# Hybrid streaming encoder on one core: the small products of the mixers' beside-work come one large product later

## The chip, the cores and the metric

The kernel runs on one core of a Trainium2 chip. The metric is the device time of one execution in microseconds (us), lower is better; a kernel's time is the median of several executions. Engines are named as the profile names them: PE (TensorE, matrix products; PEld loads its weights), DVE (VectorE), ACT (ScalarE), POOL (GpSimd), SP (the queue that issues most DMAs).

## The reference

One layer of a hybrid encoder over 2048 prompt rows and 32 rows of a running stream, all in float32, with shared weights:

```python
h = rms_norm(x, g_mix)
p = h @ w_in                              # 1024 -> 2048, eight segments of 256 columns
ya = pool_mixer(seg 0)                    # windows 2/4/8/16, mean - self, 64x64 linear
yb = conformer_conv(seg 1, seg 2)         # GLU, depthwise conv of 31 taps, LayerNorm, silu
yc = short_conv(seg 3, seg 4, seg 5)      # B * conv3(C * x)
yd = chunk_mlp(seg 6, seg 7)              # u * (tril(W_s) v + b), chunks of 128 rows
x = x + concat(ya, yb, yc, yd) @ w_out    # 1024 -> 1024
f = rms_norm(x, g_ffn)
x = x + (silu(f @ w_gate) * (f @ w_up)) @ w_down      # 1024 -> 2816 -> 1024
y = rms_norm(x, g_final)
```

It returns y and the last rows of the mixers' inputs as new states.

## The kernel before

Activations lie transposed: features on the 128 partitions, rows (tokens) along the free side. The 2080 rows make five chunks c0 to c4 of 416. Every float32 product is made of three faster ones: both operands are split into a high part (`hi`, `whi`, a cast on ACT) and the rest (`lo`, `wlo`, a subtraction on POOL or DVE), and PE adds up hi*whi, hi*wlo and lo*whi. A **large product** (`product`, L230 to L232) multiplies one chunk with one block of 128 output columns: 8 depth tiles times 3, 24 matmuls into one PSUM bank of `ps_mm` (five banks).

The chunks go through the mixers in three passes: c0; c1 and c2; c3 and c4. A pass multiplies with the column blocks of `w_in`: v (14, 15), the gated conv (`glu`, 4, 2, 5, 3), the short conv (`short`, 6, 10, 7, 11), pool (0, 1) and the gates (8, 9, 12, 13); the third pass runs in the order v, pool, glu, short, gates. Output passes with `w_out` (`w_out_pass`, eight column blocks) follow: that of c0 after the second pass, that of c1 and c2 and then that of c3 and c4 after the third. Then comes the FFN, a fast matrix scheme with fewer products (PE lines L1138 to L1155).

Beside the large products runs the rest of the mixers' work, as generators in the list `ahead`; `fill(budget)` is called once behind each large product and steps up to three of them until the budget (2.8 or 3.7 us of DVE work) is spent. A `yield` of a number is the cost of what was just issued. A `yield WAIT` ends this generator's turn until the next `fill`, so what follows it is issued at least one large product later. After `yield LATE` the generator is taken up again at the end of the same `fill`. The long conv (`taps`, 30 steps for two column halves, DVE line L727) stands in `spare` and gets what budget is left. `need(names)` runs a generator to its end at once: where a stage must have a result, all that is left is issued there, with no large product between. The order on PE and DVE is that of the program; for ACT, POOL and the DMA queues a scheduler in the compiler lays it down.

The small products of this work go to `ps_ax` (three banks):

- `spatial`: for each 128 rows, `turned` transposes v on PE (`tp`, L621) and copies it out on ACT (`vt`, L625); at the next step `mixed` multiplies it with the chunk weights (`mx`, L632) and DVE adds into `mix` (L646, and for c0 L651). A step issues `mx` of one chunk and `tp` of the next, then a WAIT.
- `pooling`: DVE builds window sums (`sa`, `sb`, L686 to L706), and `multiply` takes them through the 64x64 linear on PE (`pp`, L673).
- `normed_silu`, the LayerNorm after the long conv: `sm` on DVE (L739), `total` on PE (L743), subtract the mean on DVE (L747), squares on ACT (L756) and their sum on POOL (L757), the sums by row on PE (`tok`, L147), `ms` on DVE (L157), the power -1/2 on POOL (`rt`, L163). The scale then goes to all partitions: in the first two passes' chunks by DRAM (`spread_far`, `line` and `rs`), for c3 and c4 by PE (`dg` on DVE L168, `rb` on PE L179). DVE multiplies (L774) and ACT applies silu (L777).
- `ffn_stats`: squares of the output rows (`ssum`, ACT and DVE L347), summed by row on PE (`tok`, L147), the scales stored for the FFN. `first_operands` waits for those of c0 and c1 and then builds the FFN's first operands (DVE L993 to L1014).

`need` stands in four places that matter here: `in_pool` needs `spatial` in the first two passes; `in_short` of the third pass needs `spatial(2)`; `in_gates` needs `pooling` and `normed_silu` of chunks before; and in the output pass of c1 and c2, before its last two column blocks, `taps(2)`, `normed_silu` of c3 and c4 and `pooling(2)` are needed. The rows of x for the next chunk come by DMA (`xk`) to `normed`, which scales them on DVE (`f`, L211).

Of the kernel before, what the change touches and what calls it, by code (L numbers as in the profile page):

```python
# [58 lines left out]
def tail(p):  # L59

    lo, hi = PASSES[p][0] * C, (PASSES[p][-1] + 1) * C
    if hi <= T_PROMPT:
        return hi - lo, 0
    return T_PROMPT - lo, hi - T_PROMPT
# [21 lines left out]
def trunk_kernel(ctx: ExitStack, tc: tile.TileContext, a):  # L86
# [17 lines left out]
    def col(name, i):  # L104
        return par[:, OFF[name] + i : OFF[name] + i + 1]
# [18 lines left out]
    def row(name):  # L124
        return rowp.tile([P, C], F32, tag="row", name=name, bufs=6)
# [17 lines left out]
    def sum_tok(ssum):  # L143

        tok = ps_ax.tile([P, 512], F32, tag="ax", name="tok")
        for j in range(NTB):
            nc.tensor.matmul(  # L147
                tok[:TB, j : j + 1], ssum[:, j * TB : (j + 1) * TB], ones[:, :1], start=True, stop=True
            )
        return tok[:TB, :NTB]  # L150
# [104 lines left out]
    WAIT, LATE, DONE = object(), object(), object()  # L255
# [78 lines left out]
    def ffn_stats(c):  # L334

        acc = row("ssum")
        for ks in (range(6), range(6, KT)):
            while ks[0] and c not in whole:
                yield WAIT
            nc.sync.dma_start(  # L340
                out=x2d[:, ks[0] : ks[-1] + 1, c * C : (c + 1) * C], in_=x2[c][:, ks[0] : ks[-1] + 1]
            )
            for k in ks:
                sq = acc if k == 0 else row("sq")
                nc.scalar.activation(out=sq, in_=x2[c][:, k], func=AF.Square)
                if k:
                    nc.vector.tensor_add(out=acc, in0=acc, in1=sq)  # L347
                    yield 0.55
        made["squares", c] = True
        yield WAIT  # L350
        yield WAIT
        tok = sum_tok(acc)
        yield LATE
        rt = rsqrt_of([tok], 1.0 / D)
        yield WAIT
        nc.sync.dma_start(out=rline[c * NTB : (c + 1) * NTB].rearrange("j q -> q j"), in_=rt[:TB])
# [23 lines left out]
    with ExitStack() as st:  # L380
# [95 lines left out]
        def conv_pieces(p, h, c):  # L476
            return [(s, d - c * C + PASSES[p][0] * C, n) for s, d, n in pieces(p, h)
                    if PASSES[p][0] + d // C == c]
# [127 lines left out]
        def spatial(p, v):  # L606
            first = PASSES[p][0] * C
            n0, n1 = tail(p)
            todo = []
            t0 = first // P * P  # L610
            while t0 < first + n0:
                i0, i1 = max(first - t0, 0), min(P, first + n0 - t0)
                todo.append((HV + t0 - first, i1, i0, t0 + i0 - first))
                t0 += P
            if n1:
                todo.append((HV + n0, n1, 0, n0))

            def turned(src, k, i0, dst):
                tp = ps_ax.tile([P, 512], F32, tag="ax", name="tp")
                for t in range(2):  # L620
                    nc.tensor.transpose(  # L621
                        out=tp[:k, t * P : (t + 1) * P], in_=v[:, t, src : src + k], identity=ident
                    )
                vt = segp.tile([P, 2 * P], F32, tag="vt", name="vt", bufs=2)
                nc.scalar.copy(out=vt[:k], in_=tp[:k, : 2 * P])  # L625
                return vt

            def mixed(vt, src, k, i0, dst):
                mx = ps_ax.tile([P, 2, 2, P], F32, tag="ax", name="mx")
                n = k - i0  # L630
                for t in range(2):
                    nc.tensor.matmul(  # L632
                        mx[:, t, :, :n], vt[:k, t * P : (t + 1) * P], wst[:k, 2 * t : 2 * t + 2, i0:k],
                        start=True, stop=True,
                    )
                return mx

            def added(mx, src, k, i0, dst):
                n = k - i0
                done = 0  # L640
                while done < n:
                    c, o = PASSES[p][0] + (dst + done) // C, (dst + done) % C
                    m = min(n - done, C - o)
                    for j in range(2):
                        q = slice(64 * j, 64 * (j + 1))
                        nc.vector.tensor_add(  # L646
                            out=mix[c][q, 6:8, o : o + m], in0=mx[q, :, j, done : done + m],
                            in1=bsb[q, :, i0 + done : i0 + done + m],
                        )
                    if c == 0:  # L650
                        nc.vector.tensor_mul(  # L651
                            out=mix[c][:, 6:8, o : o + m], in0=mix[c][:, 6:8, o : o + m],
                            in1=rfirst[:, o : o + m].rearrange("p (a n) -> p a n", a=1).broadcast_to([P, 2, m]),
                        )
                    done += m

            vt = None
            for i in range(len(todo) + 1):
                mx = mixed(vt, *todo[i - 1]) if vt else None
                vt = turned(*todo[i]) if i < len(todo) else None  # L660
                yield LATE
                if mx:
                    added(mx, *todo[i - 1])
                    yield 0.7
                yield WAIT

        def pooling(p, pz):
            late = None

            def multiply(c, t, cuts, lo, sa):  # L670
                ps = ps_ax.tile([P, 512], F32, tag="ax", name="pp")
                for s, d, m in cuts:
                    nc.tensor.matmul(  # L673
                        ps[:, d : d + m], wpool[:, t], sa[:, s - lo : s - lo + m], start=True, stop=True
                    )
                nc.scalar.activation(out=mix[c][:, t], in_=ps[:, :C], func=AF.Copy, scale=col("pool_scale", t))

            for c in PASSES[p]:
                cuts = conv_pieces(p, 15, c)
                lo = cuts[0][0] - 15  # L680
                n = cuts[-1][0] + cuts[-1][2] - lo
                for t in range(2):
                    x = pz[:, t, lo : lo + n]
                    sa = segp.tile([P, 30 + C], F32, tag="sum", name="sa", bufs=2)
                    sb = segp.tile([P, 30 + C], F32, tag="sumb", name="sb")
                    nc.vector.tensor_add(out=sa[:, 1:n], in0=x[:, 1:n], in1=x[:, : n - 1])  # L686
                    yield 0.5
                    if t == 1:
                        nc.vector.tensor_add(out=sb[:, 3:n], in0=sa[:, 3:n], in1=sa[:, 1 : n - 2])
                        nc.vector.tensor_add(out=sa[:, 7:n], in0=sb[:, 7:n], in1=sb[:, 3 : n - 4])  # L690
                        yield 1.0
                    w = WINDOWS[2 * t]
                    nc.vector.tensor_add(out=sb[64:, 15:n], in0=sa[64:, 15:n], in1=sa[64:, 15 - w : n - w])
                    yield 0.5
                    fix = segp.tile([P, 15], F32, tag="fix", name="fix", bufs=2) if c == 0 else None
                    for q, s, w in ((slice(0, 64), sa, w), (slice(64, P), sb, 2 * w)):
                        if c == 0:
                            o = OFF["rc"] + 15 * t
                            nc.vector.tensor_mul(out=fix[q], in0=s[q, 15:30], in1=par[q, o : o + 15])
                            nc.vector.tensor_sub(out=fix[q], in0=fix[q], in1=x[q, 15:30])  # L700
                        nc.vector.scalar_tensor_tensor(
                            out=sa[q, 15:n], in0=s[q, 15:n], scalar=1.0 / w, in1=x[q, 15:n],
                            op0=ALU.mult, op1=ALU.subtract,
                        )
                        if c == 0:
                            nc.vector.tensor_copy(out=sa[q, 15:30], in_=fix[q])  # L706
                        yield 0.5
                    if late:
                        multiply(*late)
                    late = c, t, cuts, lo, sa  # L710
            yield WAIT
            multiply(*late)

# [21 lines left out]
        def normed_silu(p, c, cv):  # L735
            pcs = [(s - 30, d, m) for s, d, m in conv_pieces(p, 30, c)]
            sm = row("sm")
            for s, d, m in pcs:
                nc.vector.tensor_add(out=sm[:, d : d + m], in0=cv[:, 0, s : s + m], in1=cv[:, 1, s : s + m])  # L739
            yield 0.5  # L740
            yield WAIT
            total = ps_ax.tile([P, 512], F32, tag="ax", name="total")
            nc.tensor.matmul(total[:, :C], ones, sm, start=True, stop=True)  # L743
# [918 lines left out]
```

## Time and profile before

| what | value |
|---|---|
| time, median of 3 | 2114.95 us (2113.97 to 2116.43) |
| the profiled execution's own time | 2113.76 us |
| its span, first to last instruction | 2112.0 us |
| PE busy | 2028.9 us (96%), 11902 matmuls |
| DVE busy | 1451.7 us (69%) |
| ACT busy | 767.8 us (36%) |
| POOL busy | 1125.0 us (53%) |
| DMA | 247.88 MB, mean 117 GB/s |

The mixers take the first 31% of the span and the FFN the rest. Matmuls are pipelined, so a busy PE is not PE at its peak. Rows of groups read: line, engine, operation, tiles written and read, shape, count, then busy us, mean ns of one, and idle time of the engine before them with what ended it. Rows in order of time read: start, length, engine, line, operation, and in brackets the idle time just before.

### The profile page before, as it was taken

To read this page: it belongs to the slowest core of one execution; us is meant where nothing else is said; L and a number is where in the kernel's file an instruction comes from. 1 tells how busy PE (TensorE), PEld (TensorE's weight loads), DVE (VectorE), ACT (ScalarE), POOL (GpSimd) and SP (SyncE) were. 2 spreads that over 40 slices of the span, in tenths; PEclk is the share of its full clock that TensorE was granted. 3 is DMA by queue.
4 is the path that set the end of the run, shared out by engine and by line. 5 is a ranking of instruction groups with operands and counts; after the bars stand their busy time and mean duration, and the time that the engine had idled before them with its cause. 6 is when DMAs were issued, how large, how long until landed. Compare 5 with 4: busy or idle time off the path is not lost.

```text
span 2112.0 us, 31921 instructions
## 1 busy us (share of the span) xinstructions
PE 2028.9 (96%) x11902; PEld 1989.9 (94%) x11902; DVE 1451.7 (69%) x2245; ACT 767.8 (36%) x1472; POOL 1125.0 (53%) x891
## 2 busy tenths in 40 slices
PE   8799998999998999999998999999998999999997
PEld 8689997899897999999998999999998999999997
DVE  3785599499677678656557576667778576666555
ACT  5424232232334333333334343433334343433332
POOL 2433352243244666656666566655666566656664
PEclk9999998999998999999999999999999999999998
DMA  7633243213267444322223524334444524332221
GB/s 208 176 104 109 65 126 103 50 59 117 99 175 209 137 133 146 109 71 77 76 96 134 193 90 124 111 110 127 147 132 150 192 89 126 111 109 91 76 80 60
DMA packets 152011, 247.88 MB, mean 117 GB/s; under 512 B 23440, under 2 KB 101008, under 8 KB 151216
## 3 DMA queue, kind: packets, MB, share of 16 engines
q1 hardware_dynamic: 149136, 245.67, 37.9%
q8 instruction: 94, 1.54, 0.3%
q10 hardware_dynamic: 2720, 0.18, 0.1%
q14 instruction: 61, 0.50, 0.1%
HBM read 209.42 MB, written 36.36 MB: 116 GB/s over the span
## 4 chain that ended last, share of the span: by engine, by line
PE 67%; DVE 16%; DMA 6%; issue 6%; POOL 4%; ACT 1%; SPq 0%; DVEq 0%; POOLq 0%; ACTq 0%
PE pw L1140 12%; PE pw L1138 12%; PE pw L1139 12%; PE pd L1154 7%; PE pd L1155 7%; PE pd L1153 7%; DVE cv L727 5%; PE ps L232 3%; PE ps L230 3%; PE ps L231 3%; POOL wlo L1024 2%; DVE f_p L965 2%; DMA xk<-in_x 1%; DMA line<-rt 1%; DMA raw<-in_w_in 1%
## 5 line engine op out<-in xcount | busy, mean ns | idle before, releaser
L1138 PE MATMUL pw<-f_p,whi 128*128 128x346 f32 (+1 forms) x1848 | 597.7, 323 | 10.3 <-DVE sg L1231 7.4
L1140 PE MATMUL pw<-f_p,whi 128*128 128x346 f32 (+1 forms) x1848 | 598.0, 324 | 3.7 <-POOL f_p L965 3.7
L1139 PE MATMUL pw<-f_p,wlo 128*128 128x346 f32 (+1 forms) x1848 | 596.3, 323 | 0.0
L1024 POOL TENSOR_TENSOR wlo<-sum,whi 128x512 fp32r<-128x512 f32 x264 | 355.2, 1350 | 292.8 <-ACT whi L1023 284.4
L1156 DVE TENSOR_TENSOR xs<-pd,xs 128x346 f32<-128x346 f32 (+1 forms) x528 | 263.7, 513 | 243.3 <-PE pd L1155 242.7
L1138 PEld LDWEIGHTS pw<-f_p,whi 128*128 128x128 f32 x1848 | 352.3, 191 | 12.0 <-issue 8.6
L1140 PEld LDWEIGHTS pw<-f_p,whi 128*128 128x128 f32 x1848 | 350.5, 190 | 4.9 <-POOL f_p L965 4.9
L1139 PEld LDWEIGHTS pw<-f_p,wlo 128*128 128x128 f32 x1848 | 350.8, 190 | 0.3 <-POOL wlo L1024 0.3
L1153 PE MATMUL pd<-hhi,dhi 128*128 128x346 f32 (+1 forms) x1024 | 330.6, 323 | 10.1 <-DVE xs L1156 10.0
L1281 POOL TENSOR_TENSOR dlo<-raw,dhi 128x256 fp32r<-128x256 f32 x256 | 223.4, 892 | 217.7 <-ACT dhi L1280 212.4
L1154 PE MATMUL pd<-hhi,dlo 128*128 128x346 f32 (+1 forms) x1024 | 329.9, 322 | 0.0
L1155 PE MATMUL pd<-hlo,dhi 128*128 128x346 f32 (+1 forms) x1024 | 329.6, 322 | 0.0
L138 POOL TENSOR_TENSOR wlo<-raw,whi 128x1024 fp32r<-128x1024 f32 x67 | 182.4, 2726 | 271.6 <-ACT whi L137 269.9
L1024 POOL TENSOR_TENSOR wlo<-raw,whi 128x512 fp32r<-128x512 f32 x199 | 279.5, 1412 | 40.7 <-ACT whi L1023 40.7
L1023 ACT CAST whi<-sum 128x512 fp32r<-128x512 f32 x264 | 163.8, 620 | 288.9 <-DVE sum L1061 102.9
L230 PE MATMUL ps<-hi,whi 128*128 128x416 f32 x640 | 238.1, 372 | 7.4 <-ACT hi L214 3.5
L232 PE MATMUL ps<-lo,whi 128*128 128x416 f32 x640 | 233.0, 364 | 3.1 <-POOL lo L207 2.7
L231 PE MATMUL ps<-hi,wlo 128*128 128x416 f32 x640 | 230.9, 361 | 5.2 <-POOL wlo L138 4.7
L727 DVE SCALAR_TENSOR_TENSOR cv<-z,par,cv 128x416 f32<-128x416 f32 (+2 forms) x180 | 213.3, 1245 | 1.1 <-ACT cv L721 0.9
L1153 PEld LDWEIGHTS pd<-hhi,dhi 128*128 128x128 f32 x1024 | 193.4, 189 | 13.3 <-DVE xs L1156 12.2
L1155 PEld LDWEIGHTS pd<-hlo,dhi 128*128 128x128 f32 x1024 | 193.7, 189 | 0.0
L1154 PEld LDWEIGHTS pd<-hhi,dlo 128*128 128x128 f32 x1024 | 193.2, 189 | 0.4
(185 smaller groups left out, 2861.7 us busy)
## 6 DMA issues: line engine op xcount, KB each, us to landing
raw<-in_w_up SPq DMA_DIRECT2D x132, 256.0 KB
raw<-in_w_gate SPq DMA_DIRECT2D x128, 256.0 KB
raw<-in_w_down SPq DMA_DIRECT2D x256, 128.0 KB
raw<-in_w_in SPq DMA_DIRECT2D x43, 512.0 KB
raw<-in_w_out SPq DMA_DIRECT2D x24, 512.0 KB
f_p<-td SPq DMA_DIRECT2D x14, 692.0 KB
xt<-in_xt SPq DMA_DIRECT2D x20, 416.0 KB
x<-in_x SPq DMA_DIRECT2D x5, 1664.0 KB
```

Of the source, the lines that this page charges most:

```text
L230: nc.tensor.matmul(out, whi, xhi, start=start and k == 0, stop=False)
L231: nc.tensor.matmul(out, wlo, xhi, start=False, stop=False)
L232: nc.tensor.matmul(out, whi, xlo, start=False, stop=stop and k == n - 1)
L727: nc.vector.scalar_tensor_tensor(out=cv[:, t, :n], in0=z[:, t, j : j + n], scalar=col("w_conf", 31 * t + j), in1=cv[:, t, :n], op0=ALU.mul ...
L1024: nc.gpsimd.tensor_sub(out=lf, in0=src, in1=hf.bitcast(F32))
L1138: nc.tensor.matmul(ps, whi[:, k], xhi[:, k, :n], start=start and k == 0, stop=False, **more)
L1139: nc.tensor.matmul(ps, wlo[:, k], xhi[:, k, :n], start=False, stop=False, **more)
L1140: nc.tensor.matmul(ps, whi[:, k], xlo[:, k, :n], start=False, stop=stop and k == H - 1, **more)
L1153: nc.tensor.matmul(ps, whi, hhi[:, :n], start=i == 0, stop=False)
L1154: nc.tensor.matmul(ps, wlo, hhi[:, :n], start=False, stop=False)
L1155: nc.tensor.matmul(ps, whi, hlo[:, :n], start=False, stop=i == 1)
L1156: nc.vector.tensor_add(out=xs[c, m], in0=ps, in1=xs[c, m])
```

## The change

Five more `yield WAIT`, in four generators. In `ffn_stats` and `normed_silu` one more stands before the sums (`tok` of the FFN's norm, `total` of the LayerNorm), in `spatial` one more at the end of each step, in `pooling` one more before each `multiply`.

```diff
@@ ffn_stats
         made["squares", c] = True
         yield WAIT
         yield WAIT
+        yield WAIT
         tok = sum_tok(acc)
@@ spatial
                 if mx:
                     added(mx, *todo[i - 1])
                     yield 0.7
+                yield WAIT
                 yield WAIT
@@ pooling
                     if late:
+                        yield WAIT
                         multiply(*late)
                     late = c, t, cuts, lo, sa
+            yield WAIT
             yield WAIT
             multiply(*late)
@@ normed_silu
             yield 0.5
+            yield WAIT
             yield WAIT
             total = ps_ax.tile([P, 512], F32, tag="ax", name="total")
```

The new lines shift the numbers behind them by one to five (L632 is L633 in the changed kernel, L743 is L748, L777 is L782). The matmuls are the same ones; their places differ. Three places show it.

PE in the third pass, the end of `spatial(2)`. Before, its last steps stand between the products of `glu` (here the last two mixings, with a large product between that begins at `ps_3079`):

```order
L632 MATMUL mx_3047<-wst_111,vt_3006 128x256 x2
L621 MATMUL tp_3050<-ident_82,v_2535 32x128 x2
L230 MATMUL ps_3079<-hi_2185,whi_3067 128x416
...
L632 MATMUL mx_3112<-wst_111,vt_3053 128x2x32 x2
L230 MATMUL ps_3119<-hi_2185,whi_3073 128x416
```

Now `need` issues the last three mixings and two transposes in one piece, between the last product of `glu` and the first of `short` (`ps_3230`):

```order
L633 MATMUL mx_3190<-wst_111,vt_3141 128x256 x2
L622 MATMUL tp_3193<-ident_82,v_2535 128x128 x2
L633 MATMUL mx_3200<-wst_111,vt_3196 128x256 x2
L622 MATMUL tp_3203<-ident_82,v_2535 32x128 x2
L633 MATMUL mx_3210<-wst_111,vt_3206 128x2x32 x2
L230 MATMUL ps_3230<-hi_2185,whi_3218 128x416
```

In the same way four mixings and three transposes of `spatial(1)` now follow `total` in one piece before the first product of `in_pool` in the second pass.

ACT at that place of the third pass. Now the two copies that this drain needs (`vt_3196`, `vt_3206`) stand behind the silu activations of c1 and c2 (L782) and behind two DMA issues of the conv's state:

```order
L626 COPY vt_3141<-tp_3138 128x256
L782 ACT_TABLE_LOAD
L782 ACTIVATE mix_1107<-cv_1952,par_80 128x416 x2
L782 ACTIVATE mix_1106<-cv_1952,par_80 128x416 x2
L725 ACTIVATE cv_3263<-z_2845,par_80 128x862
L137 CAST whi_3378<-raw_3380 128x1024
L474 DMA out_o_conv<-z_2845 128x2x30
L475 DMA out_o_conv<-z_2845 128x2x30
L626 COPY vt_3196<-tp_3193 128x256
L725 ACTIVATE cv_3263<-z_2845,par_80 128x862
L626 COPY vt_3206<-tp_3203 32x256
```

Before, the last copy of `spatial(2)` (`vt_3053`) stood ahead of these activations.

PE in the output pass of c1 and c2, the LayerNorm of c3 and c4. Before, totals, sums and spreads each stand behind a large product of their own (two large products lie between the totals and the sums, one between the sums and the spreads):

```order
L743 MATMUL total_4140<-sm_4097,ones_87 128x416
L743 MATMUL total_4142<-sm_4100,ones_87 128x416
L230 MATMUL ps_4163<-mhi_3767,whi_4109 128x416
...
L147 MATMUL tok_4214<-ones_87,q0_4148 104x1 x4
L147 MATMUL tok_4219<-ones_87,q0_4157 104x1 x4
L230 MATMUL ps_4233<-mhi_3834,whi_4109 128x416
...
L179 MATMUL rb_4263<-dg_4260,ones_87 128x416
L179 MATMUL rb_4269<-dg_4258,ones_87 128x416
L230 MATMUL ps_4291<-mhi_3767,whi_4279 128x416
```

Now all of them stand in one piece before the same large product (`ps_4291`):

```order
L748 MATMUL total_4218<-sm_4161,ones_87 128x416
L748 MATMUL total_4220<-sm_4164,ones_87 128x416
L147 MATMUL tok_4241<-ones_87,q0_4235 104x1 x4
L179 MATMUL rb_4252<-dg_4250,ones_87 128x416
L147 MATMUL tok_4258<-ones_87,q0_4226 104x1 x4
L179 MATMUL rb_4269<-dg_4267,ones_87 128x416
L230 MATMUL ps_4291<-mhi_3759,whi_4279 128x416
```

## Prediction

> **What bounds the kernel now.** I read the page's head, then busy time by stage, who waits for whom on PE, and the chain of waits.
>
> ```profile
> span 2112.0 us, 31921 instructions
> 0.00:680.00 680.00, 631.85 (x3190) 600.86 (x3190) 505.34 (x650) 226.37 (x356) 243.89 (x140) 0.96 0.43 123
> 680.00:2112.00 1432.00, 1397.07 (x8712) 1389.05 (x8712) 946.33 (x1595) 541.40 (x1116) 881.14 (x751) 0.99 0.36 115
> ```
>
> The columns are the stretch, its length, busy time and count of PE, PEld, DVE, ACT and POOL, clock, DMA share and GB/s. The change acts almost wholly in the first 680 us, where PE is idle for 48 us. The rest is a PE-bound FFN, so what is won or lost at 680 us reaches the end. PE's waits, as total, count and longest:
>
> ```profile
> PE mx L632 <- ACT vt L625: 8.2, 3, 3.9
> PE pp L673 <- issue: 7.0, 1, 7.0
> PE pp L673 <- DVE sa L701: 4.8, 2, 4.2
> PE pw L1140 <- POOL f_p L965: 3.7, 2, 2.7
> PE tok L147 <- DVE ssum L347: 3.4, 1, 3.4
> PE total L743 <- DVE sm L739: 2.8, 1, 2.8
> ```
>
> Small products stand before 26.2 us of idle PE (8.2 + 7.0 + 4.8 + 3.4 + 2.8). That is the most the change can give back. The question is how much of it lies on the path, and what the longer beside-work costs where a stage needs its end.
>
> ```profile
> 50.00:75.00 25.00, 17.95 (x78) 15.75 (x77) 11.28 (x15) 11.69 (x21) 6.34 (x4) 0.84 0.92 226
> 75.00:100.00 25.00, 22.63 (x110) 21.56 (x110) 24.45 (x32) 9.93 (x13) 14.39 (x8) 0.93 0.43 139
> 275.00:300.00 25.00, 25.00 (x134) 24.77 (x133) 24.59 (x26) 10.47 (x15) 10.66 (x6) 1.00 0.41 118
> 450.00:475.00 25.00, 25.00 (x134) 24.77 (x133) 24.86 (x25) 7.15 (x13) 12.85 (x4) 1.00 0.27 76
> ```
>
> A large product is 24 matmuls, at 25 / 134 = 0.187 us each: 4.5 us. In the first pass (before 139 us) DMA is the limit, then DVE; in the second and third passes PE and DVE are both full.
>
> **First pass.** Its stalls go: 8.2 us before the mixings, 7.0 before a pooling product. The chain of waits (start, length, what) does not run through them:
>
> ```profile
> 54.11 13.29 DMA xk<-in_x
> 68.11 9.45 DMA xk<-in_x
> ```
>
> DVE's own row there, and two large products of PE as stretches, the first on the third chunk's rows and the last before the FFN (their edges take in two or three matmuls of the neighbours):
>
> ```profile
> 135.64 1.40 DVE L211 SCALAR_TENSOR_TENSOR f<-xk,par,rs 128x416 f32<-128x416 f32 x2 [1.16 <-DMA xk<-in_x]
> 130.26:138.75 8.49, 6.60 (x26) 4.19 (x25) 6.74 (x12) 3.76 (x8) 2.15 (x2) 1.00 0.78 230
> 654.24:658.93 4.69, 4.69 (x27) 4.65 (x26) 4.07 (x7) 1.36 (x4) 0.10 (x1) 1.00 1.06 387
> ```
>
> The chain waits for rows of x until 77.6 us, follows DVE, and waits for rows again at 135.6 us. There the first product on the third chunk takes 8.5 us (130.26 to 138.75) instead of 4.7, standing still for its operands. A PE that arrives earlier only waits longer there. So these 15.2 us are worth nothing to me. DVE gains one group of spatial adds after the rows (some 1.3 us), and one pooling product (0.9 us) moves behind that point: **+2**, bounds -15.2 (all repaid) and +3.9 (the two mixings now drained before `in_pool` stall as long as the longest did).
>
> **Second pass.** `spatial(1)` has eight chunks and nine steps. With two waits to a step, `need` before `in_pool` drains the rest: mixing, transposes, mixing and so on, with three copies by ACT between and no large product to hide them.
>
> ```profile
> L625 ACT COPY vt<-tp x19: 347/372/379, 40.6 to 400.3; 128x256 f32<-128x256 f32 x16, 32x256 f32<-32x256 f32 x2, 96x256 f32<-96x256 f32 x1
> ```
>
> A copy is 0.37 us; with its two hand-overs I put it at 0.65 (estimate): 3 x 0.65 = 2.0 at least. At most it is the 8.2 us that three such copies cost in the first pass, behind other ACT work. In ACT's new order only squares and one scaling, of some 0.5 each, stand between the copies, nearer to the lower end, so I take 3.6, less the 0.6 of the one pooling wait here: **+3** (+1.4 to +7.6).
>
> **Third pass.** The sums of squares (`tok`) come one product later, and everything behind them too. Before:
>
> ```profile
> 399.07 0.16 DVE L157 TENSOR_SCALAR ms<-tok 104x4 f32<-104x4 f32 x1 [0.57 <-PE tok L147]
> 421.76 1.09 DVE L774 TENSOR_TENSOR cv<-rs,cv 128x416 f32<-128x416 f32 x2 [9.28 <-DMA rs<-line]
> 422.77 0.58 DVE L701 SCALAR_TENSOR_TENSOR sa<-sa,pz 64x416 f32<-64x416 f32 x1
> 424.02 1.76 PE L673 MATMUL pp<-sa,wpool 128*128 128x416 f32 x2 [4.17 <-DVE sa L701]
> 434.42 0.38 ACTq L473 DMA_DIRECT2D out_o_conv<-z x1
> 434.90 0.61 ACTq L474 DMA_DIRECT2D out_o_conv<-z x1
> ```
>
> From the sums to the second chunk's scaling `L774` pass 22.7 us, since two chunks' scales go to DRAM and back one after the other. DVE is in order and stands still for it, and PE behind DVE for 4.2 us. Now three large products stand between the sums and the drain of `spatial(2)`, not four: 3 x 4.5 and three groups of small products of about 1.0 make 16.6 us. So PE is 6 us early. The drain's copy of `tp_3193` stands on ACT behind the four activations that read `L774`'s result, and behind two DMA issues that need the last `z` of the conv, which DVE makes after `L774`. From the sums: 22.7 to `L774`, 1.1 for it, 3.0 for five more DVE operations (pooling steps and `z`, 0.6 each as at 422.77), 1.0 for the two issues, 0.4 copy, then mixing, transposes, a 1.1 us activation and the last copy and mixing, some 2.3: 30.5. PE's own work in the drain is 1.5, so it stalls 30.5 - 16.6 - 1.5 = 12.4, against 4.2: **+8**. Lower bound: the copies served at once, 2.0 - 4.2 = -2.2. Upper bound +12: the clock behind the stall, too.
>
> ```profile
> 424.95:432.32 7.37, 7.37 (x27) 6.78 (x26) 7.21 (x6) 4.49 (x7) 5.54 (x2) 0.65 0.20 71
> 438.37:443.16 4.79, 4.79 (x28) 4.74 (x27) 4.79 (x6) 1.25 (x2) 0.00 (x0) 1.00 0.02 5
> 109.70:116.10 6.40, 6.40 (x27) 5.90 (x26) 6.16 (x17) 0.61 (x1) 1.04 (x2) 0.77 0.27 80
> ```
>
> A product behind a stall of 4 or 7 us takes 6.4 to 7.4 us instead of 4.8, at a granted clock of 0.65 to 0.77: 1.6 to 2.6 us a stall.
>
> **Second output pass.** DVE has the late pooling steps and adds still to do, so `taps(2)` ends about two products later, and `total` comes three later. Then `need(("normed", 3), ("normed", 4))` is upon it: totals, sums, spread, sums, spread now follow each other on PE. Prices (busy, mean ns, idle):
>
> ```profile
> L138 POOL TENSOR_TENSOR wlo<-raw,whi 128x1024 fp32r<-128x1024 f32 x2 | 4.8, 2404 | 1.6 <-issue 1.6
> L163 POOL TENSOR_TENSOR rt<-ms,mhalf 104x4 f32<-104x4 f32 x2 | 2.4, 1188 | 6.6 <-DVE ms L157 6.6
> L757 POOL TENSOR_TENSOR q<-q,q 128x416 f32<-128x416 f32 x2 | 2.1, 1093 | 6.4 <-ACT q L756 6.4
> L137 ACT CAST whi<-raw 128x1024 fp32r<-128x1024 f32 x2 | 2.1, 1045 | 10.2 <-PE ps L232 10.2
> L743 PE MATMUL total<-sm,ones 128*128 128x416 f32 x4 | 1.7, 538 | 2.8 <-DVE sm L739 2.8
> L179 PE MATMUL rb<-dg,ones 104*128 104x416 f32 x4 | 1.7, 538 | 0.3 <-DVE dg L168 0.3
> L147 PE MATMUL tok<-ones,q 128*104 128x1 f32 x16 | 1.5, 226 | 0.0
> L774 DVE TENSOR_TENSOR cv<-rb,cv 128x416 f32<-128x416 f32 x2 | 1.1, 586 | 1.0 <-PE rb L179 1.0
> ```
>
> And three rows of DVE and POOL in order of time:
>
> ```profile
> 564.38 0.59 DVE L168 TENSOR_TENSOR dg<-ident,rt 104x416 f32<-104x416 f32 x1 [0.90 <-POOL rt L163]
> 560.62 2.41 POOL L138 TENSOR_TENSOR wlo<-raw,whi 128x1024 fp32r<-128x1024 f32 x1
> 560.77 2.71 DVE L168 TENSOR_TENSOR dg<-ident,rt 104x416 f32<-104x416 f32 x1
> ```
>
> From the end of the last large product: POOL splits one weight first (cast 1.05, split 2.4, hand-overs: 3.6), adds twice 1.09 (5.8), the sums 0.8 (6.5), `ms`, `rt` and `dg` with hand-overs 1.9 (8.4), spread 0.8 (9.3), second sums 0.8 (10.1), two scalings on DVE and `ms` (10.7), `rt` and `dg` (12.4), spread (13.2). PE's own work in it is 1.7 + 1.5 + 1.7 = 4.9, so 8.3 us of stall against 2.8 + 0.3 now: +5.2; with 2.1 for the slow clock, **+7.3**. Lower bound +4.5 (no weight ahead on POOL, no slow clock). Upper bound +12: both `dg` behind a weight split, as at 560.8 us, where one took 2.71 instead of 0.59.
>
> The Trainium skill ("SBUF — State Buffer", section "Who interferes with whom") says that VectorE and GpSimd share a port pair as an exclusive lock, and that the later one blocks until the other's instruction ends; the pair of rows at 560.6 us agrees. By that rule two collisions here would add 2 x 2.1 us to this term. POOL's new order puts no split between the two `rt`, so I leave them out.
>
> **FFN's start.** The 3.4 us before `tok` go, but the waits for `f_p` (3.7 us) follow on POOL, ACT and DMA. The operands of the first FFN products begin one product later, with DVE less loaded: **-1**, bounds -3.4 and +4.5. The FFN's own small products (the final norm's) are not part of the change.
>
> Sum: 2 + 3 + 8 + 7.3 - 1 = **+19.3 us**. The profiled execution took 2113.76 us (span 2112.0 and 1.8 around it), the median is 1.2 above it: 2114.95 + 19.3 = **2134 us**.
>
> **The rivals.**
> A, not slower: the first pass is PE's own. Then every stall of `mx` and `pp` there is worth its length. It decides at the first product on the third chunk: that must start 10 us or more before 130 us and run through. Time: 19.3 - 2 - 15.2 = +2 us, 2117. For it: three stalls stand right there. Against it: DMA at 0.92 and the wait for rows at 135.6 us.
> B, much slower: the drains meet a busy ACT and POOL everywhere, so all three go to their upper bounds: 2 + 7.6 + 12 + 12 - 1 = +33, 2148. For it: both queues are in order, and the copies of the first pass did meet that.
> C, hardly slower: the third pass is DVE's (24.86 of 25 us busy at 450 us), and PE's stalls there hide in it: 2 + 3 - 1 = +4, 2119. Against it: at 421.76 us DVE waits too, and in the output pass nothing but the chain runs.
>
> **How the numbers follow.** Forecast 0.62 (2124 to 2144), B 0.16, A 0.12, C 0.10. The range reaches from A's time to B's, 2117 to 2147, and leaves out about 2 in 10. A measurement of this kernel tells some 0.2%, 4.2 us, from no change. Slower: 0.60 of the forecast, all of B, 0.03 of A and 0.03 of C: 0.82. Same: 0.02, 0.04 of A, 0.05 of C: 0.11. Faster: 0.05 of A and 0.02 of C: 0.07.
>
> **What would show it.** Right: the rows for `mx` waiting in the first pass and the 7.0 of `pp` shrink, while the first product on the third chunk still ends near 140 us; a stall of 10 us or more on PE before `short2`, with `L774` waiting for `rs` at its root; `total`, `tok`, `rb`, `tok`, `rb` with 7 to 10 us of idle PE between, in one piece before the last two output columns. Wrong: that third chunk's product ends by 130 us (A), or the last large product before the FFN ends within 5 us of its old 658.93 us.

## The result and the profile after

The changed kernel takes **2146.07 us** (median of 4: 2144.02 to 2151.91) against 2114.46 us for the kernel before beside it: ratio **1.0159**, 95% interval 1.0144 to 1.0173, so 31.6 us slower. The forecast was 2134 us, its range ended at 2147; the sign was right and the size too small by 12 us. The profiled execution took 2144.02 us with a span of 2142.3 us, 30.3 us more than before.

First the stretches, cut at the ends of the same large products in both traces. Rows of the changed kernel (columns as in the prediction):

```profile
0.00:134.73 134.73, 110.70 (x501) 100.56 (x502) 88.46 (x133) 59.08 (x99) 49.26 (x42) 0.89 0.62 180
134.73:204.35 69.62, 66.12 (x343) 63.22 (x343) 45.29 (x72) 21.62 (x38) 20.87 (x14) 0.98 0.34 101
204.35:360.17 155.82, 143.99 (x706) 137.01 (x705) 127.95 (x120) 43.10 (x58) 58.93 (x27) 0.95 0.33 94
360.17:467.94 107.77, 103.70 (x537) 98.63 (x537) 66.35 (x87) 29.30 (x50) 27.53 (x15) 0.97 0.18 55
467.94:554.49 86.55, 84.62 (x441) 82.77 (x441) 86.03 (x84) 22.03 (x30) 33.82 (x11) 0.98 0.29 95
554.49:588.70 34.21, 25.82 (x121) 23.01 (x121) 18.46 (x34) 10.33 (x20) 9.35 (x6) 0.85 0.37 122
588.70:681.55 92.85, 89.48 (x474) 88.19 (x473) 63.89 (x105) 33.24 (x51) 28.46 (x16) 0.98 0.54 171
681.55:2142.30 1460.75, 1416.16 (x8789) 1406.55 (x8787) 957.98 (x1615) 547.15 (x1126) 892.11 (x760) 0.98 0.37 115
```

| stretch, up to the end of | before, us | after, us | difference | forecast |
|---|---|---|---|---|
| first product on the third chunk | 138.75 | 134.73 | -4.0 | +2 |
| third product of `in_pool`, second pass | 63.14 | 69.62 | +6.5 | +3 |
| last v product, third pass | 151.44 | 155.82 | +4.4 | 0 |
| last product of `short2` | 107.97 | 107.77 | -0.2 | +8 |
| c1's fifth column, output pass of c1 and c2 | 83.85 | 86.55 | +2.7 | 0 |
| c1's seventh column, same pass | 26.10 | 34.21 | +8.1 | +7.3 |
| last large product | 87.68 | 92.85 | +5.2 | -1 |
| the end | 1453.07 | 1460.75 | +7.7 | (in the -1) |

Some of PE's waits in the changed kernel (total, count, longest):

```profile
PE mx L633 <- ACT vt L626: 16.0, 7, 6.3
PE ps L231 <- POOL wlo L138: 7.7, 5, 3.1
PE ps L230 <- ACT hi L214: 7.1, 4, 5.4
PE pw L1143 <- ACT f_p L966: 6.4, 2, 3.5
PE pw L1145 <- POOL f_p L970: 6.3, 2, 3.8
PE ps L230 <- DVE x L378: 6.3, 2, 3.4
PE tok L147 <- POOL q L762: 4.3, 1, 4.3
PE rb L179 <- DVE dg L168: 4.1, 2, 2.1
```

The waits of `total` and of `tok` on `ssum` are gone, and those of `pp` but for 0.6 us, as the change means. In their place `mx` waits 16.0 us instead of 8.2, the FFN waits 12.7 us for `f_p` instead of 6.6, a product of the first pass waits 5.4 us for `hi`, and one of the last large products waits 3.4 us for DVE to free a PSUM bank (`x`, L378; the other wait in this row, 2.9 us, is there before too).

### The profile page after: what moved, and what is told of

The parts are those of the page before. It is cut to its first block, busy times and chain, and to the rows that moved or that the text cites. A ratio compares the mean times of both kernels' runs of the same rounds, so it can differ in the third digit from the quotient of the medians.

```text
span 2142.3 us, 31917 instructions
## 1 busy us (share of the span) xinstructions
PE 2040.6 (95%) x11902; PEld 1999.9 (93%) x11902; DVE 1454.4 (68%) x2245; ACT 765.8 (36%) x1470; POOL 1120.3 (52%) x891
## 4 chain that ended last, share of the span: by engine, by line
PE 55%; issue 6%; DVE 5%; POOL 5%; DMA 1%; ACT 1%; POOLq 0%; DVEq 0%; SPq 0%; ACTq 0%
PE pw L1145 11%; PE pw L1143 11%; PE pw L1144 11%; PE pd L1159 6%; PE pd L1160 6%; PE pd L1158 6%; POOL wlo L1029 3%; DVE f_p L970 2%; POOL dlo L1286 1%; PE ps L230 1%; PE ps L232 1%; PE ps L231 1%; DVE x L998 1%; DMA f_p<-td 0%; DVE xs L1161 0%
## 5 line engine op out<-in xcount | busy, mean ns | idle before, releaser
L230 PE MATMUL ps<-hi,whi 128*128 128x416 f32 x640 | 238.2, 372 | 12.9 <-ACT hi L214 7.1
L731 DVE SCALAR_TENSOR_TENSOR cv<-z,par,cv 128x416 f32<-128x416 f32 (+2 forms) x180 | 218.6, 1273 | 0.6 <-ACT cv L725 0.5
L1158 PEld LDWEIGHTS pd<-hhi,dhi 128*128 128x128 f32 x1024 | 193.8, 189 | 13.2 <-DVE xs L1161 12.1
```

Source lines behind the costliest of these rows:

```text
L230: nc.tensor.matmul(out, whi, xhi, start=start and k == 0, stop=False)
L1158: nc.tensor.matmul(ps, whi, hhi[:, :n], start=i == 0, stop=False)
```

## The experiments

Three readings stood open. Why did the FFN's start cost 12.9 us and not -1? Why did the third pass cost nothing, where +8 was forecast? And are the prices of the four generators separate? Differences below are of medians to the kernel before on the same chip, or, where a stretch is named, between the same product ends of two profiled executions.

### One generator at a time

Each kernel keeps one of the diff's four parts: the extra WAIT of `ffn_stats`, of `spatial`, of `pooling` (both lines), of `normed_silu`.

> Only the WAIT of ffn_stats, on the kernel before. Theory 1 (each WAIT is paid at its own drain; the FFN's late start belongs to the later sums of squares): the first 565 us are as before, the product before the last two of the output pass waits for DVE, the FFN's first operands come late; 10 to 14 us slower, 2125 to 2129 us. Rival 2 (the late start is a DVE backlog that the LayerNorm's drain at 568 us leaves, and the sums of squares have nothing to do with it): within 2 us of before. My prediction's term of -1 would also be within 2 us.

> Only the WAIT of spatial. Theory 1: the first pass gains some 4 us at the third chunk's first product, the drain before in_pool of the second pass costs 6, and the drain of spatial(2) in the third pass stays at about 4 us: 0 to 6 us slower, 2115 to 2121 us. Rival 2 (a backlog is handed on, so the stretch before the FFN pays for what was moved earlier): over 10 us slower.

> Only the WAITs of pooling. Theory 1: the 7.0 and 4.8 us that PE stood before a pooling product shrink, the first pass hides most of it: 0 to 5 us faster, 2110 to 2115 us. Rival 2 (pooling's later steps add to DVE's backlog in the output pass, since pooling(2) is drained there too): 2 to 6 us slower.

> Only the WAIT of normed_silu. Theory 1: the third pass loses nothing, the totals, sums and spreads of c3 and c4 come in one piece before the last two output columns and cost 8 us; the FFN's start is as before: 7 to 12 us slower, 2122 to 2127 us. Rival 2 (the late FFN start is the backlog that this drain leaves): 18 to 24 us slower, 2133 to 2139 us.

| part | us | ratio (95%) | `in_pool` stretch | to `short2`'s end | c1's 7th column | last large product | FFN |
|---|---|---|---|---|---|---|---|
| ffn_stats | 2125.93 | 1.0053 (1.0036 to 1.0070) | 0.0 | -1.4 | -1.1 | +4.3 | +7.4 |
| spatial | 2141.33 | 1.0127 (1.0099 to 1.0155) | +6.9 | **+12.7** | **+12.0** | +0.3 | +2.4 |
| pooling | 2113.07 | 0.9993 (0.9983 to 1.0003) | +0.7 | -0.8 | +5.0 | 0.0 | +0.4 |
| normed_silu | 2116.54 | 1.0013 (1.0003 to 1.0022) | 0.0 | **-7.1** | +6.3 | 0.0 | +1.9 |

Three of the eight stretches are left out; in them the differences lie between -4.8 and +3.9 us.

`ffn_stats` alone gives the stall before the last large product and the FFN's late start: theory 1. For `spatial` both theories fall. The size is that of rival 2, but the place isn't: not a handed-on backlog, but +12.7 at its own drain in the third pass, as the prediction had feared there, and +12.0 in the output pass, which neither theory had. `pooling` alone makes no measurable difference, as theory 1 allows; the +5.0 at c1's seventh column, where rival 2 looked for a loss, does not show in the time. `normed_silu` costs 2 us and not 7 to 12: it pays 6.3 us at c1's seventh column, but gains 7.1 us in the third pass. So it hides there the loss that `spatial` makes; that is the -0.2 of the whole change. The four sum to 38.5 us, the whole is 31.6; the four times of `spatial` alone spread over 11 us, so this difference shows little. The stretches show more: at c1's seventh column the four sum to +22.0, and the whole change pays +8.1. There they are not independent: they share one drain.

### The FFN's start

Before and after, DVE's first scaling of FFN operands that waits for c1's scales, and the four adds that free PSUM banks behind the operands' work:

```profile
616.37 1.78 DVE L993 SCALAR_TENSOR_TENSOR x<-x,par,rs 128x416 f32<-128x416 f32 x3 [1.59 <-DMA rs<-rline]
641.34 2.08 DVE L377 TENSOR_TENSOR x<-ps,x 128x416 f32<-128x416 f32 x4
```

```profile
640.60 1.78 DVE L998 SCALAR_TENSOR_TENSOR x<-x,par,rs 128x416 f32<-128x416 f32 x3 [3.85 <-DMA rs<-rline]
665.41 2.07 DVE L378 TENSOR_TENSOR x<-ps,x 128x416 f32<-128x416 f32 x4
```

`need(("first", 0))` drains these operands on DVE between two column pairs, and the adds stand behind it. The scaling comes 24.2 us later where PE is 17.4 us late (c1's seventh column ends at 588.70 instead of 571.25 us): 6.8 us have gone into c1's sums and the round trip of its scales. PE, done with the product before, has no free bank for the next:

```profile
666.13 0.43 PE L230 MATMUL ps<-mhi,whi 128*128 128x416 f32 x1 [3.37 <-DVE x L378]
```

Which chunk's sums do it?

```diff
         made["squares", c] = True
         yield WAIT
         yield WAIT
+        if c == 1:          # e5; c > 2 in e9
+            yield WAIT
         tok = sum_tok(acc)
```

> The WAIT of ffn_stats for c1 alone, on the kernel before; the sums of c0, c2, c3 and c4 keep their places. Theory 1: first_operands waits for c1's sums, so all of the 11 us that the WAIT of ffn_stats cost for all chunks comes back: 9 to 13 us slower, 2124 to 2128 us. Rival 2: the late sums of c3 and c4 beside the first FFN products cost it; then this is within 3 us of before.

> The WAIT of ffn_stats for c3 and c4 alone. Theory 1 (two separate prices: c1's later sums hold PSUM banks before the last output product, c3's later sums put the store of their scales in front of the last operand's load on SP's queue): no stall before the last large products, the FFN's first products wait for f_p and weights: 4 to 9 us slower, 2117 to 2121 us. Rival 2 (the FFN's late operands need the delay by c1 too): within 2 us of before.

c1 alone: 2117.15 us, ratio 1.0028 (1.0017 to 1.0039), half of what theory 1 asked. c3 and c4 alone: 2120.34 us, 1.0029 (1.0016 to 1.0043), 6.5 us slower and in theory 1's range. PE's waits from 640 us on, first with c1's WAIT, then with those of c3 and c4 (its four largest):

```profile
PE pw L1140 <- ACT f_p L963: 4.3, 1, 4.3
PE tok L147 <- DVE ssum L347: 4.2, 1, 4.2
PE pw L1142 <- POOL f_p L967: 3.5, 3, 2.3
PE ps L230 <- DVE x L379: 2.5, 1, 2.5
```

```profile
PE pw L1142 <- POOL f_p L967: 6.9, 2, 4.0
PE pw L1140 <- ACT f_p L963: 6.2, 2, 3.3
PE pw L1141 <- POOL wlo L1026: 2.5, 3, 1.0
PE pw L1140 <- ACT whi L1025: 1.7, 2, 1.4
```

So there are two prices, in two places. c1's sums take the bank (+4.2 us up to the last large product, +1.4 in the FFN); c3's and c4's sums, which stand between the FFN's first products, make `f_p` and the weights late (+0.9 and +5.6; 13.1 us of waits for `f_p`, 6.6 before). 4.2 + 1.4 + 0.9 + 5.6 = 12.1, against 4.3 + 7.4 = 11.7 for the whole WAIT of `ffn_stats`. On SP's queue the changed kernel has the store of c3's scales between the loads of the last two operands, where before it stood ahead of both:

```
before:                                     after:
L356 DMA rline_103<-rt_5201 104x4x1         L964 DMA f_p3_5236<-td_4427 128x1392
L959 DMA f_p3_5237<-td_4427 128x1392        L357 DMA rline_103<-rt_5234 104x4x1
L959 DMA f_p4_5266<-td_4428 128x1392        L964 DMA f_p4_5257<-td_4428 128x1392
L356 DMA rline_103<-rt_5264 104x4x1         L357 DMA rline_103<-rt_5320 104x4x1
```

That this order alone makes the 5.6 us was not tried apart.

The other direction, c1's sums one product sooner than before (`if c != 1:` ahead of the second WAIT):

> The other direction: c1 has one WAIT fewer than before in ffn_stats, so its sums come one large product sooner. Theory 1: DVE's work on the first FFN operands starts about 5 us sooner, and the waits for f_p at the FFN's start (3.7 and 2.9 us before) shrink: 2 to 7 us faster, 2108 to 2113 us. Rival 2: the FFN's start hangs on something else (the last rows' sums, the weights): within 2 us of before.

2119.09 us, ratio 1.0035 (1.0023 to 1.0047): slower, a miss for both theories. DVE took the early sums only at 605.25 us (604.16 before), since it was still adding squares; and the load of the last column pair's weights came to stand behind more operand stores on SP, so the product before the last two waited 3.7 us for its weight. Earlier was no gain here.

The whole change without this WAIT:

> The whole change without the WAIT of ffn_stats. Theory 1: the 11 to 13 us that this WAIT costs alone are missing and nothing else moves: 2132 to 2137 us, where the whole change takes 2146. Rival 2 (the prices of the WAITs overlap, since one waits in the shadow of the other): 2139 to 2146 us.

2138.22 us, ratio 1.0117 (1.0100 to 1.0133): 24.4 us slower than before, 7.2 us less than the whole change, between the theories. The stretch to the last large product keeps +0.0 behind c1's seventh column and the FFN +1.2, so the two prices are gone; the drain before that column is 1.2 us dearer and `in_pool`'s 2.1 us.

### The third pass: two round trips in series

POOL and SP before, each in order of time, from the sums (their second `ms` at 399.07 us) to the second scaling (421.76 us):

```profile
398.58 1.02 POOL L163 TENSOR_TENSOR rt<-ms,mhalf 104x4 f32<-104x4 f32 x1 [2.58 <-DVE ms L157]
399.57 2.39 POOL L138 TENSOR_TENSOR wlo<-raw,whi 128x1024 fp32r<-128x1024 f32 x1
401.92 1.01 POOL L163 TENSOR_TENSOR rt<-ms,mhalf 104x4 f32<-104x4 f32 x1
399.62 0.33 SPq L185 DMA_DIRECT2D line<-rt  x1
405.93 0.34 SPq L187 DMA_DIRECT2D rs<-line  x1
406.83 0.36 SPq L185 DMA_DIRECT2D line<-rt  x1
417.96 0.32 SPq L187 DMA_DIRECT2D rs<-line  x1
```

The same in the changed kernel, with DVE's scaling and a weight split that ran beside it:

```profile
406.86 0.16 DVE L157 TENSOR_SCALAR ms<-tok 104x4 f32<-104x4 f32 x1 [0.57 <-PE tok L147]
406.37 2.00 POOL L163 TENSOR_TENSOR rt<-ms,mhalf 104x4 f32<-104x4 f32 x2 [1.86 <-DVE ms L157]
407.41 1.30 SPq L185 DMA_DIRECT2D line<-rt  x2
413.92 0.82 SPq L187 DMA_DIRECT2D rs<-line  x2
418.89 4.18 DVE L779 TENSOR_TENSOR cv<-rs,cv 128x416 f32<-128x416 f32 x4
418.71 2.40 POOL L138 TENSOR_TENSOR wlo<-raw,whi 128x1024 fp32r<-128x1024 f32 x1 [10.35 <-ACT whi L137]
```

Before, POOL splits a weight between the two `rt`, so the first chunk's read, which SP issues in order and only when its write has landed, stands ahead of the second chunk's write: that write's `rt` is done at 402.93 us, and it is issued at 406.83. The trips follow each other. The second write also takes longer to land: SP waits 10.7 us for it and 5.9 for the first; why is open. Now both writes go first and both reads overlap. From the second `ms` to the second chunk's scaling are 22.7 us before and 15.1 now (421.99 us, the third of the four scalings), and DVE waits for no read: the four scalings follow its own work, and the first of them takes 2.68 us beside the weight split. The prediction took the 22.7 of before for a fixed time.

The claim is that `spatial`'s drain stalls for this trip. With `spatial`'s WAIT, and `normed_silu`'s for c1 and c2 only (`if p == 1: yield WAIT`):

> The WAIT of spatial together with that of normed_silu for c1 and c2. Theory 1: the long stall of spatial's drain in the third pass (8.7 and 5.4 us of PE before two mixings with spatial's WAIT alone) hangs on the two round trips in series; with the reads side by side it falls to some 4 us, and the kernel is 10 to 16 us faster than with spatial's WAIT alone: 2125 to 2131 us. Rival 2: the drain stalls by itself, on ACT's copies: 2136 to 2142 us, as with spatial's WAIT alone.

And with the trip taken away, the sums left where they were:

```diff
-            if p < 2:
+            if p < 1:
                 rb = spread_far(rt)
```

> The same with spatial's WAIT in all passes. Theory 1: the sums stand where they stood with spatial's WAIT alone (2141 us), but nothing waits for DRAM, so the drain of spatial(2) stalls little: 10 to 16 us faster than that, 2125 to 2131 us. Rival 2 (the drain stalls since the sums come before it, on ACT's queue): 2136 to 2142 us.

PE's waits between 405 and 450 us, with `spatial`'s WAIT alone, then without the trip:

```profile
PE mx L632 <- ACT vt L625: 14.6, 3, 8.7
```

```profile
PE mx L632 <- ACT vt L625: 5.4, 2, 4.9
```

With the trips side by side (e8) PE waits 4.1 us there, as in the whole change, and the kernel takes 2128.55 us, ratio 1.0077 (1.0062 to 1.0092): theory 1. Without them (e14) the stretch to `short2`'s end costs +3.7 instead of +12.7, and the kernel takes 2132.84 us, 1.0093 (1.0072 to 1.0114), 8.5 us less than with `spatial`'s WAIT alone, a little short of the 10 that theory 1 asked and outside its range. Both point the same way: some 9 to 10 of the 14.6 us are the DRAM trips in series, seen through DVE and ACT, and 4 to 5 us belong to the drain itself.

The same on the kernel before, without any WAIT added:

> The WAIT of normed_silu for c1 and c2 alone. Theory 1: in the third pass the two writes of the scales to DRAM come right behind each other and their two reads overlap, so the second chunk's scaling comes sooner and PE's stall before short2 goes; the totals of c3 and c4 keep their places, so the drain in the output pass costs nothing: 7 to 10 us faster, 2105 to 2108 us. Rival 2: whatever comes earlier there is given back in the output pass, as with the WAIT for all chunks: within 3 us of before.

> On the kernel before, no WAIT added: the scales of c1 and c2 go to all partitions by PE (diagonal and ones, as for c3 and c4) instead of by DRAM. Theory 1 (the stall before short2 is made by the two round trips in series): DVE no longer stands 9.3 us for the read, PE's stall of 4.2 us and the slow product behind it go, two diagonals and two spreads are added: 4 to 9 us faster, 2105 to 2110 us. Rival 2 (the stall is DVE's own work): within 3 us of before.

`normed_silu`'s WAIT for c1 and c2 alone: **2107.44 us, ratio 0.9982** (0.9973 to 0.9991), between the theories; the stretch to `short2`'s end gains 5.5 us, and c1's seventh column costs 0.1. Spreading by PE: **2106.32 us, ratio 0.9964** (0.9954 to 0.9974), 8.3 us faster than before, as theory 1 had it, and the lowest median of the study. That it beats the WAIT is not shown: the two intervals touch, and behind the first pass its profiled execution gains 4.2 us, that of the WAIT 5.0. DVE's scaling there no longer waits for a read, and PE's 4.2 us before `pp` are gone:

```profile
410.54 2.07 DVE L774 TENSOR_TENSOR cv<-rb,cv 128x416 f32<-128x416 f32 x4
```

Adding `pooling`'s WAITs to `normed_silu`'s for c1 and c2:

> The WAIT of normed_silu for c1 and c2 together with the WAITs of pooling. Theory 1: both took away the same stall before short2 in the third pass, so pooling adds at most the 2 us it had alone: 3 to 8 us faster than before, 2107 to 2112 us. Rival 2 (pooling's later steps reach the drain in the output pass): 0 to 5 us slower than before.

2109.05 us, 0.9982 (0.9971 to 0.9993): in theory 1's range, and rival 2 is out. That the two take the same stall is not shown: up to `short2`'s end this kernel gains 7.1 us, against 5.5 and 0.8 for the two alone.

### The output pass and the second pass

PE in the output pass of the changed kernel, in order of time, and DVE's two diagonals:

```profile
567.92 1.56 PE L748 MATMUL total<-sm,ones 128*128 128x416 f32 x4
573.74 0.89 PE L147 MATMUL tok<-ones,q 128*104 128x1 f32 x8 [4.26 <-POOL q L762]
576.70 1.72 PE L179 MATMUL rb<-dg,ones 104*128 104x416 f32 x2 [2.07 <-DVE dg L168]
578.22 1.43 PE L147 MATMUL tok<-ones,q 128*104 128x1 f32 x8
```

```profile
575.97 0.59 DVE L168 TENSOR_TENSOR dg<-ident,rt 104x416 f32<-104x416 f32 x1 [1.13 <-POOL rt L163]
580.97 0.59 DVE L168 TENSOR_TENSOR dg<-ident,rt 104x416 f32<-104x416 f32 x1 [1.12 <-POOL rt L163]
```

The stall is 4.26 + 2.07 + 2.06 = 8.4 us (8.3 forecast). With `normed_silu`'s WAIT in all passes PE waits 6.4 us here for the diagonals; with it for c1 and c2 only it waits 2.9 us for `sm`, as before; with `pooling`'s WAITs alone it waits 5.3 us for `sm`:

```profile
PE rb L179 <- DVE dg L168: 6.4, 2, 4.6
```

```profile
PE total L745 <- DVE sm L739: 2.9, 1, 2.9
```

```profile
PE total L745 <- DVE sm L741: 5.3, 1, 5.3
```

So the drain's price hangs on where c3's and c4's totals stand and when DVE has `sm` ready. In PE's order the totals are one product later with the WAIT of `spatial` alone and with that of `normed_silu` alone, and the diagonals then stall PE 6.4 us in both; `spatial` adds 3.4 us of waiting for `sm`, and the granted clock of the stretch is 0.78 (+12.0). With `pooling` alone the totals keep their place, and only the wait for `sm` grows (+5.0, clock 0.89). In the whole change the totals are three products later.

The +4.4 of the third stretch was in no term. Of it, 3.3 us have come by the end of `in_glu`, and they belong to c0's LayerNorm; the rest is open. (In the second pass `glu` runs behind `in_pool`.) In the changed kernel DVE waits for c0's scales, the next `ms` waits behind, POOL's `rt` for it, and a weight split behind that:

```profile
211.76 1.09 DVE L779 TENSOR_TENSOR cv<-rs,cv 128x416 f32<-128x416 f32 x2 [9.37 <-DMA rs<-line]
213.02 1.29 POOL L163 TENSOR_TENSOR rt<-ms,mhalf 104x4 f32<-104x4 f32 x1 [10.12 <-DVE ms L157]
214.28 2.34 POOL L138 TENSOR_TENSOR wlo<-raw,whi 128x1024 fp32r<-128x1024 f32 x1
```

The second product of `glu` waits 3.1 us for that split (the longest in the list of waits) and runs slow behind it. With `normed_silu`'s WAIT alone the same wait is 2.9 us and the stretch to the end of `in_glu` is +4.2; with the WAIT for c1 and c2 only, which leaves c0 alone, it is -0.7.

### The first pass

```diff
+                if p == 0:
+                    yield WAIT
                 yield WAIT
```

> The WAIT of spatial in the first pass alone. Theory 1 (first pass bound by rows of x and DVE up to 139 us, as the prediction had it): between 2 us faster and 4 us slower, 2112 to 2118 us. Rival 2 (the first pass is PE's own and the stalls of its mixings are repaid): 6 to 8 us faster, 2104 to 2108 us.

2113.29 us, ratio 1.0000 (0.9988 to 1.0012): the time that theory 1 gave. But the stalls did not go: `mx` waits 10.5 us there, against 8.2 before, so this run does not tell what their going would be worth. In the whole change they did not go either. PE's two longest waits up to 140 us there, and the first stretch before:

```profile
PE mx L633 <- ACT vt L626: 8.4, 2, 6.3
PE ps L230 <- ACT hi L214: 5.7, 2, 5.4
```

```profile
0.00:138.75 138.75, 114.52 (x503) 103.30 (x504) 86.96 (x132) 59.44 (x100) 51.83 (x42) 0.90 0.63 174
```

`pp`'s 7.0 us are gone, and a wait for `hi` has come: PE stands idle for 24.2 us of this stretch before (138.75 - 114.52) and for 24.0 now (134.73 - 110.70). The product ahead of the third chunk's first ends at 118.2 us instead of 130.4; the first itself then waits 5.4 us for `hi`, takes 11.1 us, and ends only 4.0 us sooner. With `pooling`'s WAITs alone `pp` waits 2.6 us and `hi` 4.8 us, at a ratio of 0.9993.

## Why the prediction was right or wrong

- **First pass, +2: right that its stalls are worth nothing, but not as reckoned.** "Its stalls go" is half wrong: `pp`'s 7.0 us went, `mx`'s 8.2 stayed (8.4, at the drain before `in_pool`, which the upper bound had). What went came back at the third chunk's first product, as "a PE that arrives earlier only waits longer there" says: PE came there 12 us sooner and left it 4.0 us sooner. Rival A (2117) is out: that product did not run through. The -4.0 in the profile is no gain that could be shown: with before's own, eight profiled executions have before's order of PE up to there, and their first product on the third chunk ends between 133.99 and 140.25 us. The +2 itself can't be told from this scatter.
- **Second pass, +3 (bounds +1.4 and +7.6): mechanism right, size too small.** +6.5 measured here, +6.9 with `spatial` alone, +4.0 in e8, +8.5 in e10. The drain's copies stalled PE 3.5 us (69.62 - 66.12; 3.6 reckoned); the term left out the clock behind the stall: PE is busy 3.0 us longer there than before (66.12 against 63.14). PE waits 3.2 or 3.3 us in the three others; the granted clock is 1.00 in e8, 0.98 here, 0.95 with `spatial` alone and 0.94 in e10, in the order of the prices.
- **Third pass, +8: the step failed.** "Two chunks' scales go to DRAM and back one after the other" is true of before and not of after: write, read, write, read on SP's queue has become write, write, read, read. The prediction read POOL's new order for the output pass and made no use of it, nor of SP's, here. So its sign, a stall of 10 us or more before `short2`, did not come: PE waits 4.1 us there, about what it waited before (4.2). With `spatial` alone, where the trips stay in series, the stall is 14.6 us, against 12.4 reckoned.
- **Second output pass, +7.3: right,** +8.1 measured, with the totals three products later and the stall as reckoned. Both diagonals took 0.59 us. No weight split ran beside them, so the two collisions that the Trainium skill's rule ("SBUF — State Buffer", section "Who interferes with whom") would have charged did not occur, as argued.
- **FFN's start, -1 (bounds -3.4 and +4.5): the step that failed, and threw the sum out.** +12.9 measured, +11.3 by e1's median. "One product later, with DVE less loaded" left out the `need` of the first operands, which the four places of `need` named ahead of the prediction do not have either: DVE drains them in one piece, with the adds that free PSUM banks behind (3.37 us of PE). It also took c3's and c4's sums for free, and they cost some 6.5 us (0.9 + 5.6).
- **In no term:** +4.4 behind the second pass, 3.3 of it by c0's LayerNorm (shown by e4 against e7). The +2.7 before the output drain goes with the wait for the first `mlo` (1.85 us, 0.3 before), and that stretch moves by -1.5 to +4.8 among the experiments, also where nothing there was changed; its cause stays open.
- **Rivals B and C:** the time is near B's 2148, but not by B's way: none of its three upper bounds was reached (6.5 of 7.6, -0.2 of 12, 8.1 of 12), and the FFN was not in it. C's sum (2119) is out.

The misses add up, in us of the profiled executions: -6.0 in the first pass and -8.2 in the third, +3.5 in the second, +4.4 behind it, +2.7, +0.8 in the output pass and +13.9 at the FFN's start: 11.1. Misses of 14.2 us one way hide 25.3 the other way; that the sum came within 12 us is in part luck.

## What to carry to other kernels

A piece of work moved later by one slot was paid for here where its last consumer is drained in one piece, so list every such drain, with the adds that free buffers behind it, before costing any move. The wait for a round trip was here not a property of the transfer alone but of the order on the queues that issue it: read the changed order of SP and POOL before reusing the old duration. And where a trip to DRAM only spreads a few numbers to all partitions, price the same on PE.

## What the runs showed that was not expected

- The first 139 us move by themselves: with the same order of PE up to there, the first product on the third chunk ends between 133.99 us (`normed_silu` alone) and 140.25 us (c1's sums early).
- Four scalings on DVE, the first of which ran while POOL split a weight for 2.40 us, took 4.18 us (rows at 418.89 and 418.71): 2.68 us the first and 0.58 each of the others. With `normed_silu`'s WAIT alone, and no split beside them, the same four took 2.09. This agrees with the Trainium skill's rule named above, at a place where the prediction had not looked for it.
- Three stalls of 4.26, 2.07 and 2.06 us within 15 us went with a mean granted clock of 0.85 over a 34.21 us stretch (1.00 before, with 2.8 and 0.3 us of stalls). The same waits don't always cost it: in the second pass's drain, e8 (3.2 us in three waits) keeps 1.00, `spatial` alone (3.3 us in three) has 0.95.
